# A reversed second token block, and a convolution DFT on sums and differences of the two blocks

## The chip, the cores and the metric

The kernel runs on one core of a Trainium2 chip. The metric is the device time of one execution in microseconds (us), the median of the runs. All of the work on tensors is on the device; the host only lays out the inputs, among them tables of sines and cosines, and puts the output's rows in order.

## The reference, cut to what matters

One decoder layer with 256 tokens of width 1024: RMS norm, an input projection, attention with 8 heads beside a convolution branch of 512 channels, an output projection with a residual, a second RMS norm and a SwiGLU of width 2816 with a residual. The change is in the convolution branch:

```python
def conformer_conv(u, glu_b, dw_w, dw_b, ln_g, ln_b):
    u = u + glu_b.astype(u.dtype)
    a, g = jnp.split(u, 2, axis=-1)
    h = a * jax.nn.sigmoid(g)
    h = jnp.pad(h, ((0, 0), (CONV_KERNEL - 1, 0), (0, 0)))
    h = lax.conv_general_dilated(
        h, dw_w[:, None, :].astype(h.dtype), window_strides=(1,), padding='VALID',
        dimension_numbers=('NWC', 'WIO', 'NWC'), feature_group_count=CONV_WIDTH)
    h = h + dw_b.astype(h.dtype)
    h = layer_norm(h, ln_g, ln_b)
    return jax.nn.silu(h)
```

It is a causal convolution with 31 taps along the tokens, for each channel by itself.

## The kernel before, in words

The tokens lie on the 128 partitions in two blocks: tokens 0 to 127 and 128 to 255. Every float32 product is made of three matmuls: an operand is split into a rounded high part and a low part (`split`, L207: ScalarE copies the high part, VectorE subtracts for the low one), and `mm3` (L318 to L321) adds high·high, high·low and low·high into one PSUM bank. A weight arrives in blocks of 2048 columns (`raw`) and is split piece by piece, 1024 columns each: `feed` (L275) issues the high part `wh` of a piece on ScalarE (L279) one piece ahead of the low part `wl` on VectorE (L227), and after the low part of an odd piece it loads a new block on SyncE's queue (L205). There is one stream of instructions for each engine, in the order of the program text; nothing is put in another order later. Generators (`spawn`, `step`) weave the side work into the matmul stream: one `step` for each group of six matmuls, and `yield n` means "go on n steps later". The constants at the top say how many steps.

The input projection (L739) runs over five chunks of 512 columns: k, q, the convolution's gate, the convolution's values, v. `conv_task` (L619) starts behind the fourth chunk and works beside the fifth. It forms the gated input `ua0`, `ua1` of the two blocks, splits them into `hh`, `hl`, and multiplies by `fwd`: a DFT of 256 tokens at odd frequencies whose cosine half goes to the bank `hf0` and whose sine half to `hf1` (`spectrum`, L637), each over both blocks. A third, short transform `hf2` takes block 1 alone: the wrapped-around part of the circular convolution is put right with it. `combine` multiplies by the spectra `Ws` of the taps, giving `Y0`, `Y1`; `Y2` comes from `hf2`. `ln_task` (L674) goes back with `inv`: one bank `cv` for each block, over Y0 and Y1, and Y2 for block 0. Then come the mean and variance (`bn_stats`), an inverse square root by small VectorE steps (`lr`, `nb`), `yn` on ScalarE, the transposes `cT` (L714), SiLU, and the split into `mix`, which the output projection `po` (L785) reads.

Beside this runs attention. For each head h there are scores `S`, a masked maximum `sm`, `bi` (VectorE), the exponentials `p` (ScalarE, L591), `rec` (VectorE), a scaling by GpSimd (L599), three transposes into a bank `pT` (L603) and a copy `pTs` out of it (ScalarE, L605). `pT` and `hf2` take turns in the two PSUM banks of the tag "t" (L158); `S` of heads 6 and 7, `hf0`, `hf1` and `cv` in the two of the tag "s". After head 7's exponentials ScalarE loads the table for SiLU (L594). Behind the chunks come `vs`, the values of v scaled (block 0 on ScalarE, L746, block 1 on VectorE, L747), the short transform (`third`, L658), and the products `O` of all heads (L759, L760), which need `vs` and the `pTs`.

After the output projection, `x2_task` (L788) adds the residual, transposes (`xT`, L801) and makes the next operand `g` (L807, L809), which the gate and up products `fg`, `fu` read (L308, L310).

Of the kernel before, what the change touches and what calls it, by code (L numbers as in the profile page):

```python
# [82 lines left out]

def _constants():


# [4 lines left out]
    c, s = waves(T, np.arange(T))  # L91
    ct, st = waves(2 * LAGS, np.arange(P) - (P - LAGS))
    fwd = np.concatenate([c[:P], s[:P], c[P:], s[P:], np.where(np.arange(P)[:, None] < P - LAGS, 0.0,
                                                              np.concatenate([ct, st, ct, st], 1))], 1)
# [47 lines left out]
def _build(nc, tc, t, ctx):  # L142
# [476 lines left out]
    def conv_task(banks):  # L619
        hh = early.tile([P, NT, W], F32R, name="hh", tag="hh")  # L620
        hl = early.tile([P, NT, W], F32R, name="hl", tag="hl")
        us = []
        for i in range(NT):
# [3 lines left out]
            nc.scalar.activation(hh[:, i, :], u, AF.Copy)  # L627
# [4 lines left out]
        nc.vector.tensor_tensor(hl[:, 1, :], us[1], hh[:, 1, :].bitcast(F32), op=ALU.subtract)  # L632
# [471 lines left out]
```

## Time and profile before

| what | us |
|---|---|
| median of 3 runs | 284.97 (284.8 to 285.31) |
| the profiled execution, first to last instruction (span) | 283.1 |
| TensorE busy / weight loads | 278.5 / 234.3 |
| VectorE busy | 239.0 |
| ScalarE busy | 207.8 |
| GpSimd busy | 47.7 |

The page of the profile gives no time of its own for the profiled execution beside its span. The median of the runs is 1.9 us above that span: what lies before the first and after the last instruction, and the scatter of the runs.

How to read the rows: PE is TensorE's matmuls, PEld its weight loads, DVE VectorE, ACT ScalarE, POOL GpSimd, SPq SyncE's DMA queue. A row of the timeline has the start, the length, engine, line, operation, output<-inputs, shapes and a count, and in brackets the idle time ahead of it with what ended that. A row of the chain has start, length, what. An instruction can show a start before its forerunner's end, since they are pipelined: the distance from start to start is what one of them costs in a row of them. Granted TensorE clock is 1.000 throughout.

### The profile page before, as it was taken

The page shows a single profiled execution, that of the slowest core. Times are in us where ns is not written, and L with a number is a line of the kernel's source. Part 1 is how long each engine was busy: PE and PEld are TensorE (multiplying, and loading weights), DVE is VectorE, ACT ScalarE, POOL GpSimd, SP SyncE. Part 2 cuts the span into 40 slices and gives each one's busy share as a digit, 9 for nine tenths or more (in the row PEclk, how much of TensorE's full clock was granted, in tenths as well). Part 3 has the DMA queues.
Part 4 walks back from the last instruction along what each step waited for, and adds up shares of the span by engine and source line. Part 5 has one row for each costly group of instructions (what it writes and reads, how often), then busy time and mean ns, then how long its engine had stood idle before and what let it go on. Part 6 is the DMA issues. An engine that isn't in the chain of part 4 may idle for free.

```text
span 283.1 us, 4174 instructions
## 1 busy us (share of the span) xinstructions
PE 278.5 (98%) x1463; PEld 234.3 (83%) x1463; DVE 239.0 (84%) x425; ACT 207.8 (73%) x336; POOL 47.7 (17%) x75
## 2 busy tenths in 40 slices
PE   8999999999999999999999999999999999999994
PEld 6788887788788888888888888888888888888883
DVE  3979996996894869999967687698789879999995
ACT  4858579996738677467878778776678799888770
POOL 0004556623000000000111111000011211211233
PEclk9999999999999999999999999999999999999999
DMA  7999957845203982659699998995686969999643
GB/s 247 396 425 354 420 191 275 328 160 214 85 7 141 362 316 78 287 163 394 202 291 280 304 318 228 285 274 171 243 213 167 242 183 258 321 311 207 190 74 148
DMA packets 13638, 69.03 MB, mean 244 GB/s; under 512 B 1777, under 2 KB 2385, under 8 KB 7730
## 3 DMA queue, kind: packets, MB, share of 16 engines
q1 hardware_dynamic: 10162, 56.19, 53.0%
q0 software_dynamic: 3312, 12.58, 22.1%
q8 instruction: 11, 0.18, 0.2%
q14 instruction: 9, 0.07, 0.1%
q10 hardware_dynamic: 144, 0.00, 0.0%
HBM read 66.15 MB, written 2.10 MB: 241 GB/s over the span
## 4 chain that ended last, share of the span: by engine, by line
PE 97%; DMA 1%; ACT 0%; DVE 0%; issue 0%
PE p L739 20%; PE sum L968 18%; PE fg L308 14%; PE fu L308 14%; PE po L785 8%; PE fg L310 7%; PE fu L310 7%; DMA first<-first 1%; PE S L561 1%; PE pT L603 1%; PE O L759 1%; PE xT L801 1%; PE cv L319 0%; PE cv L320 0%; PE hf L319 0%; PE cv L321 0%
## 5 line engine op out<-in xcount | busy, mean ns | idle before, releaser
L279 ACT ACTIVATE wh<-raw 128x1024 fp32r<-128x1024 f32 x81 | 83.9, 1053 | 15.3 <-PE fu L308 7.5
L227 DVE TENSOR_TENSOR wl<-raw,wh 128x1024 fp32r<-128x1024 f32 x63 | 75.9, 1219 | 3.4 <-ACT wh L279 3.3
L308 PE MATMUL fu<-g,wh 128*128 128x512 f32 x176 | 62.5, 395 | 0.0
L308 PE MATMUL fg<-g,wh 128*128 128x512 f32 x176 | 62.4, 394 | 0.0
L310 PE MATMUL fg<-g,wl 128*128 128x256 f32 x176 | 48.8, 277 | 0.0
L310 PE MATMUL fu<-g,wl 128*128 128x256 f32 x176 | 48.8, 277 | 0.0
L308 PEld LDWEIGHTS fg<-g,wh 128*128 128x128 f32 x176 | 33.0, 187 | 7.8
L308 PEld LDWEIGHTS fu<-g,wh 128*128 128x128 f32 x176 | 33.0, 188 | 7.6
L225 POOL DMA_DIRECT2D wl<-w x18 | 15.8, 876 | 138.2 <-ACT wl L224 74.3
L310 PEld LDWEIGHTS fg<-g,wl 128*128 128x128 f32 x176 | 33.0, 188 | 0.0
L310 PEld LDWEIGHTS fu<-g,wl 128*128 128x128 f32 x176 | 33.0, 188 | 0.0
L968 PE MATMUL sum<-wh,forms 128*128 128x512 f32 x96 | 29.6, 389 | 0.0
L739 PE MATMUL p<-wh,xh 128*128 128x512 f32 x80 | 25.7, 403 | 0.1
L739 PE MATMUL p<-wl,xh 128*128 128x512 f32 x80 | 24.8, 391 | 0.0
L739 PE MATMUL p<-wh,xl 128*128 128x512 f32 x80 | 24.7, 390 | 0.0
L279 ACT ACTIVATE wh<-t 128x1024 fp32r<-128x1024 f32 x18 | 19.1, 1059 | 6.0 <-DVE t L242 3.3
L227 DVE TENSOR_TENSOR wl<-t,wh 128x1024 fp32r<-128x1024 f32 x17 | 20.8, 1223 | 1.2 <-ACT wh L279 0.8
L968 PEld LDWEIGHTS sum<-wh,forms 128*128 128x128 f32 x96 | 17.9, 188 | 3.7
L224 ACT ACTIVATE wl<-wh 128x1024 fp32r<-128x1024 f32 x19 | 20.2, 1062 | 0.6
L968 PE MATMUL sum<-wl,forms 128*128 128x512 f32 x48 | 18.7, 389 | 0.0
L739 PEld LDWEIGHTS p<-wl,xh 128*128 128x128 f32 x80 | 14.9, 188 | 3.4 <-DVE wl L388 0.3
L739 PEld LDWEIGHTS p<-wh,xl 128*128 128x128 f32 x80 | 15.0, 188 | 3.3
(208 smaller groups left out, 475.6 us busy)
## 6 DMA issues: line engine op xcount, KB each, us to landing
raw<-w SPq DMA_DIRECT2D x44, 1024.0 KB, 6.8
wl<-w POOLq DMA_DIRECT2D x18, 512.0 KB, 9.5
first<-first SPq DMA_DIRECT2D x8, 384.0 KB, 6.3
raw<-w SPq DMA_DIRECT2D x2, 512.0 KB, 7.1
xtok<-xtok SPq DMA_DIRECT2D x2, 512.0 KB, 9.1
x<-xtok SPq DMA_DIRECT2D x2, 512.0 KB, 6.7
kept<-x POOLq DMA_DIRECT2D x1, 1024.0 KB, 4.1
raw<-kept SPq DMA_DIRECT2D x1, 1024.0 KB, 7.4
```

Source lines behind the costliest of these rows:

```text
L224: nc.scalar.activation(dst[1], dst[0].bitcast(F32), AF.Copy, scale=-1.0)
L225: nc.gpsimd.dma_start(dst[1], src.bitcast(F32R), accum_op=ALU.add)
L227: nc.vector.tensor_tensor(dst[1], src, dst[0].bitcast(F32), op=ALU.subtract)
L279: nc.scalar.activation(dst[0], src, AF.Copy)
L308: nc.tensor.matmul(out.rearrange("p (a q) -> p a q", a=2), w[0], both, start=z in first and z not in seen, stop=False)
L310: nc.tensor.matmul(out[:, 0:T], w[1], both[:, 0, :], start=False, stop=z in last and left[z] == 0)
L561: nc.tensor.matmul(banks[a][:, out], G["qT"][rows, j, q], G["kT"][rows, j, k], start=True, stop=True)
L603: nc.tensor.transpose(b[:, a * P:(a + 1) * P], p[:, a * P:(a + 1) * P], ident)
L739: nc.tensor.matmul(banks[i], (xh, xh, xl)[a][:, kt, sls[i]], w[a % 2], start=kt == 0 and a == 0, stop=kt == KT - 1 and a == 1)
L759: nc.tensor.matmul(o, vs[:, 0, hs], G["pT"][h][:, 0:T], start=True, stop=False)
L785: nc.tensor.matmul(po[i, n], G["mix"][l][:, k, i * P:(i + 1) * P], w[r], start=k == a == 0, stop=k == KT - 1 and a == 2)
L968: nc.tensor.matmul(banks[m], lhs, rhs, start=first, stop=last)
```

## The change

The tokens of block 1 are laid out in the order 128, 255, 254 ... 129 (`_turned`), in x, in the rotation table, in the mask and, on the host, in the output. Row r of block 1 (r from 1) then holds token 256-r, for which the DFT's cosines are those of token r with the sign changed and its sines the same. So the cosine half needs only the difference `ue` of the blocks and the sine half only their sum `uo` (row 0 apart: the columns `keep` and `minus` are 0 there). Forward there are three products of three matmuls, back three more, and the blocks are put together from `cv0` (even) and `cv1` (odd) on VectorE. That is 18 matmuls where there were 30.

```diff
-PT_WAIT = (4, 5, 3, 3)
+PT_WAIT = (4, 5, 5, 3)
-LN_WAIT = 2
+LN_WAIT = 3
-V_PIECE = 21
+V_PIECE = 22
...
+def _turned(a):
+
+    return np.concatenate([a[:P + 1], a[:P:-1]], 0)
...
     def conv_task(banks):
-        hh = early.tile([P, NT, W], F32R, name="hh", tag="hh")
-        hl = early.tile([P, NT, W], F32R, name="hl", tag="hl")
+        hh = early.tile([P, 3, W], F32R, name="hh", tag="hh")
+        hl = early.tile([P, 3, W], F32R, name="hl", tag="hl")
+        low = lambda j, u: nc.vector.tensor_tensor(hl[:, j, :], u, hh[:, j, :].bitcast(F32), op=ALU.subtract)
...
-            nc.scalar.activation(hh[:, i, :], u, AF.Copy)
             us.append(u)
-            if i:
-                nc.vector.tensor_tensor(hl[:, 0, :], us[0], hh[:, 0, :].bitcast(F32), op=ALU.subtract)
             yield 1
-        nc.vector.tensor_tensor(hl[:, 1, :], us[1], hh[:, 1, :].bitcast(F32), op=ALU.subtract)
+        ue, uo = work("ue", "tmp", 6), work("uo", "tmp", 6)
+        nc.vector.scalar_tensor_tensor(ue, us[1], G["minus"], us[0], op0=ALU.mult, op1=ALU.add)
+        nc.scalar.activation(hh[:, 0, :], ue, AF.Copy)
+        nc.vector.scalar_tensor_tensor(uo, us[0], G["keep"], us[1], op0=ALU.mult, op1=ALU.add)
+        nc.scalar.activation(hh[:, 1, :], uo, AF.Copy)
+        low(0, ue)
+        low(1, uo)
         yield HF_WAIT
...
-            for i in range(NT) if j < 2 else (1,):
-                o = i * T + j * P if j < 2 else 2 * T
-                mm3(b[:n, :], [f[:, o:o + n] for f in fwd], (hh[:, i, :], hl[:, i, :]), i == 0 or j == 2, i == NT - 1)
+            mm3(b[:n, :], [f[:, o:o + n] for f in fwd], (hh[:, j, :], hl[:, j, :]), True, True)
...
         combine(0)()
+        nc.scalar.activation(hh[:, 2, :], us[1], AF.Copy)
+        low(2, us[1])
         second = combine(1)
...
     def ln_task():
-        for i in (1, 0):
-            b = t_bank(f"cv{i}", "s")
-            for j in range(2):
-                o = j * T + i * P
-                mm3(b, [m[:, o:o + P] for m in inv], G["ys"][j], j == 0, i == 1 and j == 1)
-            if i == 0:
-                mm3(b, [m[:TAIL + 1, 2 * T:] for m in inv], G["ys"][2], False, True)
-                cv[i] = b
-            else:
-                cv[i] = work("cvb", "tmp", 6)
-                nc.vector.tensor_tensor(cv[i], b, G["glub"][:, 2, :], op=ALU.add)
+        for j in (1, 0, 2):
+            b = sums[j] = t_bank(f"cv{j}", "s" if j < 2 else "t")
+            n = TAIL + 1 if j == 2 else P
+            mm3(b, [m[:n, j * P:(j + 1) * P] for m in inv], G["ys"][j], True, True)
+        odd, even, late = (work(f"cv{a}", "tmp", 6) for a in "oel")
+        nc.vector.tensor_tensor(odd, sums[1], G["glub"][:, 2, :], op=ALU.add)
+        nc.scalar.activation(even, sums[0], AF.Copy)
+        nc.vector.scalar_tensor_tensor(late, even, G["minus"], odd, op0=ALU.mult, op1=ALU.add)
+        nc.vector.scalar_tensor_tensor(even, odd, G["keep"], even, op0=ALU.mult, op1=ALU.add)
+        nc.vector.tensor_tensor(even, sums[2], even, op=ALU.add)
+        cv = [even, late]
+        for i in (1, 0):
             nc.vector.bn_stats(st[:, i, :], cv[i])
             nc.vector.bn_aggr(mv[:, i, :], st[:, i, :])
-            if i:
-                feed(V_PIECE + 1)
```

The tables `fwd` and `inv` shrink from 1264 and 1280 columns to 752 and 768; the small table `cols` grows from 16 to 18. `V_PIECE` is the last piece whose low part is made during the v chunk. The order of the instructions moves at three places; the lines of the changed kernel are 6 to 14 higher than before.

TensorE from the first transform to the products O, before (`p40` is the v chunk's bank for block 0, six matmuls a group; `pT4` is head 4's bank):

```order
L321 MATMUL hf0_807<-hh_676,fwd_434 128x512
L603 MATMUL pT4_814<-c_ident_165,p4_712 128x128 x3
L603 MATMUL pT5_820<-c_ident_165,p5_721 128x128 x3
L739 MATMUL p40_662<-wh18_613,xh_110 128x512
...
L319 MATMUL hf1_836<-hh_676,fwd_434 128x512
...
L739 MATMUL p40_662<-wh19_642,xh_110 128x512
...
L603 MATMUL pT6_858<-c_ident_165,p6_778 128x128 x3
L603 MATMUL pT7_864<-c_ident_165,p7_791 128x128 x3
...
L319 MATMUL hf2_880<-hh_676,fwd_434 120x512
...
L759 MATMUL O0_895<-pTs0_668,vs_876 64x256
```

The same place with the change:

```order
L327 MATMUL hf0_811<-hh_676,fwd_434 128x512
L753 MATMUL p40_662<-wh18_613,xh_110 128x512
...
L325 MATMUL hf1_825<-hh_676,fwd_434 128x512
...
L753 MATMUL p40_662<-wh19_642,xh_110 128x512
...
L610 MATMUL pT4_850<-c_ident_165,p4_711 128x128 x3
L610 MATMUL pT5_856<-c_ident_165,p5_720 128x128 x3
L610 MATMUL pT6_862<-c_ident_165,p6_782 128x128 x3
L610 MATMUL pT7_868<-c_ident_165,p7_795 128x128 x3
...
L325 MATMUL hf2_884<-hh_676,fwd_434 120x512
...
L773 MATMUL O0_899<-pTs0_668,vs_880 64x256
```

`hf0` and `hf1` have three matmuls instead of six, and the transposes of heads 4 and 5 have moved two groups later, right ahead of those of heads 6 and 7. The four `pT` take turns in two banks.

ScalarE from head 7's last exponential to `vs`, before (`wh22` is the high part of weight piece 22):

```order
L591 ACTIVATE p7_791,sums_507<-sm7_750,bi7_754,scq_432 128x256
L594 ACT_TABLE_LOAD
L594 ACTIVATE table_76<-const-float32-1.0 128x1
L279 ACTIVATE wh22_795<-raw11_582 128x1024
L605 ACTIVATE pTs4_818<-pT4_814 128x384
L605 ACTIVATE pTs5_824<-pT5_820 128x384
```

With the change:

```order
L598 ACTIVATE p7_795,sums_507<-sm7_754,bi7_758,scq_432 128x256
L601 ACT_TABLE_LOAD
L601 ACTIVATE table_76<-const-float32-1.0 128x1
L285 ACTIVATE wh22_799<-raw11_582 128x1024
L285 ACTIVATE wh23_829<-raw11_582 128x1024
L667 ACTIVATE hh_676<-ua1_723 128x512
L612 ACTIVATE pTs4_854<-pT4_850 128x384
L612 ACTIVATE pTs5_860<-pT5_856 128x384
```

`wh23`, which came later in `ln_task`, and the third split's high part now stand between the table load and the copies `pTs4`, `pTs5`.

VectorE from the low part of piece 21 to `Y1`, before (`ya`, `yb` are the two products of `combine`):

```order
L227 TENSOR_TENSOR wl21_757<-raw10_493,wh21_756 128x1024
L597 RECIPROCAL rec7_826<-sums_507 128x2
L651 TENSOR_TENSOR ya0_849<-hf0_807,Ws_503 128x512
L652 TENSOR_TENSOR yb0_850<-hf1_836,Ws_503 128x512
L653 TENSOR_TENSOR Y0_544<-ya0_849,yb0_850 128x512
L651 TENSOR_TENSOR ya1_854<-hf0_807,Ws_503 128x512
L652 TENSOR_TENSOR yb1_855<-hf1_836,Ws_503 128x512
L747 TENSOR_SCALAR vs_876<-p41_663,c_176 128x512
L653 TENSOR_TENSOR Y1_545<-ya1_854,yb1_855 128x512
```

With the change:

```order
L233 TENSOR_TENSOR wl21_761<-raw10_493,wh21_760 128x1024
L604 RECIPROCAL rec7_815<-sums_507 128x2
L233 TENSOR_TENSOR wl22_800<-raw11_582,wh22_799 128x1024
L662 TENSOR_TENSOR ya0_839<-hf0_811,Ws_503 128x512
L663 TENSOR_TENSOR yb0_840<-hf1_825,Ws_503 128x512
L664 TENSOR_TENSOR Y0_544<-ya0_839,yb0_840 128x512
L629 TENSOR_TENSOR hl_677<-ua1_723,hh_676 128x512
L662 TENSOR_TENSOR ya1_846<-hf0_811,Ws_503 128x512
L663 TENSOR_TENSOR yb1_847<-hf1_825,Ws_503 128x512
L761 TENSOR_SCALAR vs_880<-p41_663,c_176 128x512
L664 TENSOR_TENSOR Y1_545<-ya1_846,yb1_847 128x512
```

`wl22` (from `ln_task`) and the third `hl` now stand ahead of `vs`. Earlier on VectorE, `ue` and `uo` stand between `ua1` and the first two `hl`, and the maxima of heads 6 and 7 follow those. Six matmuls of the output projection move from behind the transposes `cT` to ahead of them (36 instead of 30 ahead, 42 instead of 48 between `cT` and `xT`).

More of the change, by code (lines that the diff above doesn't have):

```diff
@@ L89, in waves @@
         return np.cos(ang), -np.sin(ang)
[L91 to L94, printed above, removed]
+    row = np.arange(P)
+    c, _ = waves(T, row)
+    _, s = waves(T, np.where(row == 0, P, row))
+    ct, st = waves(2 * LAGS, LAGS - row)
+    fwd = np.concatenate([c, s, np.where((row < 1) | (row > LAGS), 0.0, np.concatenate([ct, st, ct, st], 1).T).T], 1)
     fwd = _parts(fwd.astype(np.float32))
-    ir, ii = waves(2 * LAGS, np.arange(P) + LAGS)
-    tail = np.concatenate([ir, -ir, ii, ii], 1).T / LAGS * (np.arange(P) < LAGS)
-    tail = np.concatenate([tail, np.ones((1, P)), np.zeros((P - TAIL - 1, P))], 0)
+    ir, ii = waves(2 * LAGS, row + LAGS)
+    tail = np.concatenate([ir, -ir, ii, ii], 1).T / LAGS * (row < LAGS)
+    tail = np.concatenate([tail, (row == 0)[None], np.zeros((P - TAIL - 1, P))], 0)
     inv = _parts(np.concatenate([c.T * 2 / T, s.T * 2 / T, tail], 1).astype(np.float32))
@@ L107, in _constants @@
     out = {"fwd": fwd, "inv": inv, "taps": taps}
-    q, k = np.arange(P)[:, None], np.arange(P)[None, :]
-    tri = np.where(k <= q, 0.0, -1e30)
-    out["mask"] = np.concatenate([tri, np.zeros((P, P)), tri], 1).astype(np.float32)
+    at = _turned(np.arange(T))
+    tri = [np.where(b[None, :] <= b[:, None], 0.0, -1e30) for b in (at[:P], at[P:])]
+    out["mask"] = np.concatenate([tri[0], np.zeros((P, P)), tri[1]], 1).astype(np.float32)
     out["ident"] = np.eye(P, dtype=np.float32)
@@ L452, in tables_task @@
         G["glub"] = load(early, "rows", [P, 3, W])
-        G["cols"] = load(const, "cols", [P, 16])
+        G["cols"] = load(const, "cols", [P, 18])
+        G["keep"], G["minus"] = G["cols"][:, 16:17], G["cols"][:, 17:18]
     def spectra_task():
@@ L542, in q_task @@
         nc.gpsimd.tensor_scalar(G["scq"], cqk[0], HD ** -0.5, None, op0=ALU.mult)
-        for name, shape in (("fwd", [P, 2, 2 * T + TAIL]), ("inv", [P, 2, 2 * T + P])):
+        for name, shape in (("fwd", [P, 2, 2 * P + TAIL]), ("inv", [P, 2, 3 * P])):
             tl = early.tile(shape, F32R, name=name)
@@ L679, in ln_task @@
         vv = early.tile([P, NT], F32, name="vv")
-        for i in (1, 0):
-            b = t_bank(f"cv{i}", "s")
-            for j in range(2):
-                o = j * T + i * P
-                mm3(b, [m[:, o:o + P] for m in inv], G["ys"][j], j == 0, i == 1 and j == 1)
-            if i == 0:
-                mm3(b, [m[:TAIL + 1, 2 * T:] for m in inv], G["ys"][2], False, True)
-                cv[i] = b
-            else:
-                cv[i] = work("cvb", "tmp", 6)
-                nc.vector.tensor_tensor(cv[i], b, G["glub"][:, 2, :], op=ALU.add)
+        sums = {}
+        for j in (1, 0, 2):
[9 more added lines that the diff above has]
+        cv = [even, late]
+        for i in (1, 0):
             nc.vector.bn_stats(st[:, i, :], cv[i])
             nc.vector.bn_aggr(mv[:, i, :], st[:, i, :])
-            if i:
-                feed(V_PIECE + 1)
         nc.vector.tensor_scalar(vv, mv[:, :, 1], EPS, None, op0=ALU.add)
@@ L1053, in _layout @@
     A = {k: np.asarray(v) for k, v in a.items()}
-    x = A["x"][0]
+    x = _turned(A["x"][0])
     w_in = A["w_in"][0]
@@ L1081, in _layout @@
         "g1": colize(A["norm1_g"][0]),
-        "cols": np.concatenate([colize(A["norm2_g"][0]), colize(A["conv_ln_g"][0]), colize(A["conv_ln_b"][0])], 1),
+        "cols": np.concatenate([colize(A["norm2_g"][0]), colize(A["conv_ln_g"][0]), colize(A["conv_ln_b"][0]),
+                                np.outer(np.arange(P) > 0, np.float32([1, -1]))], 1).astype(np.float32),
         "rows": rep(np.concatenate([A["glu_b"][0].reshape(2, W), A["dw_b"]], 0)),
@@ L1102 @@
     o = np.asarray(r.results[0]["out"])
-    return np.ascontiguousarray(o).reshape(1, T, D)
+    return np.ascontiguousarray(_turned(o)).reshape(1, T, D)
```

5 lines of the change are left out of this document (2 added, 3 removed).

## Prediction

> **What bounds the kernel now.** I read the page's busy times first, then what TensorE waits for, then the chain that ended last, and then the timelines of TensorE, VectorE and ScalarE around the convolution.
>
> From the page, and from the view of TensorE's waits, its only row:
>
> ```profile
> PE 278.5 (98%) x1463; PEld 234.3 (83%) x1463; DVE 239.0 (84%) x425; ACT 207.8 (73%) x336; POOL 47.7 (17%) x75
> PE warm L370 <- PEq L1095: 0.8, 1, 0.8
> ```
>
> TensorE is busy for 98% of the span and stands idle for nothing but the warm-up's start. So the span of before is TensorE's stream, and any change ends it earlier by what it takes out of that stream, less the waits that it puts in. The chain of waits, between 60 and 106 us, shows the stretch in question (start, length, what):
>
> ```profile
> 63.01 0.23 PE hf L319
> ...
> 69.89 1.37 PE p L739 x6
> ...
> 74.92 0.43 PE cv L319
> ...
> 78.39 0.23 PE cv L321
> 78.63 6.83 PE po L785 x30
> 85.46 0.87 PE cT L714 x8
> 86.33 10.93 PE po L785 x48
> 97.26 0.87 PE xT L801 x8
> ...
> 105.94 0.32 PE fg L308
> ```
>
> One matmul of the transforms costs 0.233 us in the stream (14 steps from 74.92, its first a little longer, to 78.39: 0.23 each), one of the output projection 6.83/30 = 0.228, a group of six of the v chunk 1.37.
>
> **What the change takes out.** Twelve transform matmuls at 0.233 make 2.80 us, 1.40 in `hf` and 1.40 in `cv`. If TensorE stayed the bound, that would be the gain, whole. [...] The stage at hand tells another story, by the view of busy times from the end of `ua1` to two us past `vs` (stretch, length, then PE, PEld, DVE, ACT, POOL busy with their counts, the granted clock, and DMA):
>
> ```profile
> 59.68:74.10 14.42, 14.42 (x88) 11.88 (x88) 11.54 (x28) 11.45 (x26) 4.12 (x8) 1.00 0.47 181
> ```
>
> VectorE has 14.42 - 11.54 = 2.9 us free here, and the change brings `ue`, `uo` (about 0.65 each in a row), the third `hl` (0.60) and `wl22` (1.12): 3.0 us. The room is just used up if nothing waits. So the question is what waits.
>
> **VectorE's slip at the split.** The timelines of VectorE and ScalarE before:
>
> ```profile
> 58.21 0.74 DVE L625 SCALAR_TENSOR_TENSOR ua<-p,c,c_rows 128x512 f32<-128x512 f32 x1
> 58.99 0.69 DVE L626 TENSOR_TENSOR ua<-ua,sgt 128x512 f32<-128x512 f32 x1
> ...
> 60.42 0.69 DVE L632 TENSOR_TENSOR hl<-ua,hh 128x512 fp32r<-128x512 f32 x1
> ...
> 62.97 1.22 DVE L227 TENSOR_TENSOR wl<-raw,wh 128x1024 fp32r<-128x1024 f32 x1
> ...
> 64.18 1.20 DVE L227 TENSOR_TENSOR wl<-raw,wh 128x1024 fp32r<-128x1024 f32 x1
> 64.11 0.15 DVE L597 RECIPROCAL rec<-sums 128x2 f32<-128x2 f32 x1
> 65.30 0.15 DVE L597 RECIPROCAL rec<-sums 128x2 f32<-128x2 f32 x1
> ...
> 67.89 0.69 DVE L652 TENSOR_TENSOR yb<-hf,Ws 128x512 f32<-128x512 f32 x1 [1.85 <-PE hf L321]
> 68.62 0.69 DVE L653 TENSOR_TENSOR Y<-ya,yb 128x512 f32<-128x512 f32 x1
> 69.23 0.68 DVE L651 TENSOR_TENSOR ya<-hf,Ws 128x512 f32<-128x512 f32 x1
> ...
> 71.30 0.75 DVE L747 TENSOR_SCALAR vs<-p,c 128x512 f32<-128x512 f32 x1 [0.79 <-PE p L739]
> ```
>
> ```profile
> 59.78 0.61 ACT L627 ACTIVATE hh<-ua 128x512 fp32r<-128x512 f32 x1
> 60.30 1.05 ACT L279 ACTIVATE wh<-raw 128x1024 fp32r<-128x1024 f32 x1
> ...
> 62.33 0.49 ACT L591 ACTIVATE p<-sm,bi,scq 128x128 f32<-128x128 f32 x1 [0.24 <-DVE bi L586]
> ...
> 64.59 1.28 ACT L594 ACT_TABLE_LOAD   x1
> 65.88 0.20 ACT L594 ACTIVATE table<-const-float32-1.0 128x1 f32<-128x1 f32 x1
> 65.99 1.05 ACT L279 ACTIVATE wh<-raw 128x1024 fp32r<-128x1024 f32 x1
> 66.94 0.85 ACT L605 ACTIVATE pTs<-pT 128x384 f32<-128x384 f32 x2
> ```
>
> `ua1` ends at 59.68. `ue` follows at 59.72 (0.04 from end to start, as L625 to L626). No row has this operation from SBUF alone; the nearest are L625, which reads PSUM (0.74), and L626 (0.69), and I take 0.71. Then `hh0` on ScalarE (0.61, from 60.47), `uo` meanwhile to 61.09, `hh1` to 61.74, and only then the second `hl`, at 61.78 and not 60.42: a slip of 1.36 us. Behind it stand the `rec` and the maxima of heads 6 and 7, whose exponentials waited for VectorE already (the bracket at 62.33). So all of ScalarE's row slips by 1.36: table load 67.22 done, `wh22` at 67.35, done at 68.40.
>
> **VectorE's wait for `wh22`.** VectorE is through `rec7` at 65.45 + 1.36 = 66.81, then stands at `wl22`, which needs `wh22`: it starts at 68.44, a new wait of some 1.6 us. Behind it: `ya0` 1.12 later (64.18 to 65.30) at 69.56, `yb0` 0.60, `Y0` 0.73 (67.89 to 68.62), `hl` 0.61, then three steps of 0.60 to `vs` at 73.30, which ends at 74.05. Before it ended at 71.30 + 0.75 = 72.05: 2.00 later. The products `O` need it from their second matmul on, and `cv` follows `O`. With the first product already through, I take `cv` 1.95 us later than 74.92, give or take 0.4.
>
> **TensorE meanwhile** has its own new wait, and it is covered by this one. `hf0` must also wait until the maximum has read head 6's bank (0.2). `pT4` then comes at 63.01 + 0.2 + 2 x 0.70 + 2 x 1.37, about 67.4, and `pT5` is through 0.66 later; `pT6` needs `pT4`'s bank, so the copy `pTs4`, which stands behind `wh22`, `wh23` (0.95 from start to start, 65.99 to 66.94) and `hh` (0.52, 59.78 to 60.30): from 69.77 to 70.24. TensorE stands there for 2.2 us, finishes `hf2` near 73.1 and waits once more, 0.9, for `vs`. Were this first wait gone, `vs` would still be late.
>
> **At the output projection**: +1.95 - 1.40 (the six `cv` matmuls) = **+0.55**. Beside the `po` matmuls runs the way to `yn`:
>
> ```profile
> 76.56 0.69 DVE L690 TENSOR_TENSOR cvb<-cv,c_rows 128x512 f32<-128x512 f32 x1 [0.28 <-PE cv L321]
> ...
> 82.34 0.16 DVE L698 SCALAR_TENSOR_TENSOR nb<-mv,lr 128x2 f32<-128x2 f32 x1
> ...
> 83.22 0.80 ACT L703 ACTIVATE yn<-cvb,nb,lr 128x512 f32<-128x512 f32 x1
> ```
>
> From the first addition to `nb` it took 82.50 - 76.56 = 5.94, with one `wl` of 1.12 in it, and 1.52 more to the end of `yn`. That `wl` is gone, and three operations of some 0.73 are added (two to put the blocks together, one for the third bank). It starts once `O` is split, about 1.3 (a `hh`-like copy and a subtraction) behind its end near 76.9: 78.2 + 5.94 - 1.12 + 2.2 + 1.52 = 86.7. `cT` is due at 85.46 + 0.55 + 6 x 0.228 = 87.38. So this work costs nothing, with 0.6 to spare; beyond that each us would count.
>
> **Behind `cT`** it has slipped by 0.55 + 1.37 = 1.92, and what hangs on it is tight:
>
> ```profile
> 89.27 0.69 DVE L209 TENSOR_TENSOR mixl<-cs,mixh 128x512 fp32r<-128x512 f32 x1 [0.88 <-ACT mixh L208]
> 89.88 5.76 DVE L227 TENSOR_TENSOR wl<-raw,wh 128x1024 fp32r<-128x1024 f32 x5
> 95.56 1.28 DVE L791 TENSOR_TENSOR x<-po,x 128x512 f32<-128x512 f32 x2
> ...
> 105.22 1.66 DVE L809 SCALAR_TENSOR_TENSOR g<-xT,c_cols,g 128x256 fp32r<-128x256 f32 x4 [1.77 <-ACT g L807]
> ```
>
> From `mixl` to the residual VectorE has no idle time, and 42 matmuls instead of 48 lie over it. The residual ends at 96.84 + 1.92 = 98.76; `xT`'s second half would be due at 97.26 + 0.43 + 0.55 = 98.24: a wait of about 0.5. The same holds at the second `xT`, and the fifth `g` (ready 105.22 + 0.42 = 105.64, used at 105.94) has 0.30 of slack. So the end slips by 1.92 - 0.30 = **+1.6**. Behind that the trace of before shows TensorE without a wait.
>
> **Edits at nothing.** The smaller tables come on GpSimd's queue at 45 us, far ahead of their use at 63 and 75; `cols` has two columns more; the row order is the host's. Piece 23's low part and the block load behind it on SyncE's queue come at 86.4 instead of 83.6:
>
> ```profile
> 83.66 12.34 SPq L205 DMA_DIRECT2D raw<-w  x4
> raw<-w SPq DMA_DIRECT2D x44, 1024.0 KB, 6.8
> ```
>
> The block lands 6.8 later, at 93.2; ScalarE reads it as the last of five high parts, near 94.9 with its own slip. Covered by 1.7; uncovered, it would delay the weights of the gate product.
>
> **The sum** against the profiled execution: -2.80 of matmuls, +3.35 of waits ahead of `cv` (1.95 + 1.40), +1.05 from `xT` on: 283.1 becomes 284.7. The runs' median is 1.9 above that span, and nothing is changed at either end: 284.97 + 1.6 = 286.6.
>
> **The rivals.**
>
> *The second half is hidden* (chance 0.20). For: the slacks behind `cT` come from single rows. Against: three places in a row are tight. Then only +0.55 is left: 285.5, with 285.0 to 285.9.
>
> *VectorE's new work fits its free time* (0.18), the case on the other side. Place: `wl22`. If `wh22` is done by the time VectorE has passed `rec7`, near 66.7, the 1.6 us of wait and most of the slip go, `vs` ends within 0.2 us of before, and `po` starts 1.2 earlier. Against: `wh22` stands behind the table load, and that behind VectorE itself. And the chain behind `cT` would take back up to 1.1 of it. 283.7 to 284.8.
>
> *TensorE stays the bound* (0.06), -2.80: 282.2. The 2.9 us of free time against 3.0 of new work and two waits speak against it.
>
> *The clock falls in the new gap* (0.06). The stretch above shows a granted clock of 1.00, but TensorE has no wait in it. If the 2.2 us ahead of `pT6` brought it to half, the nine matmuls up to `O` would take twice their 0.23, 2.1 more, of which the 0.9 of waiting for `vs` hides a part: +1.2 on the forecast, 287.8. [...]
>
> **How the numbers follow.** The forecast keeps 0.50, with 285.9 to 287.4 as its own range (0.4 of `vs`, 0.3 of slack). The range 284.1 to 287.5 takes in the forecast, the hidden second half and two thirds of the fitting case; left out are that case's last third, the full gain and the fallen clock, 0.06 each. A measurement of this kernel tells about 0.2% from no change, 0.57 us. Slower by more than that: the forecast, the fallen clock and half of the hidden case, 0.66. Faster by more: two thirds of the fitting case and the full gain, 0.18. Within: the rest of these two cases, 0.16.
>
> **What would show it.** In the profile after: `wl22` on VectorE with an idle time of 1 to 2 us ahead of it that ScalarE's `wh` ends; `vs` on VectorE ending near 74; TensorE with a row of waits for `pTs` or `vs`, and one at `xT`; `po` starting near 79.2, `cT` near 87.4. The forecast is wrong if TensorE shows no waits between 63 and 106 us, or if `po` starts before 78.

## The result and the profile after

| kernel | median of 6 runs, us | lowest and highest | ratio to before |
|---|---|---|---|
| before | 284.97 | 284.8 to 285.45 | |
| changed | 287.0 | 286.73 to 288.8 | 1.0088 (95% interval 1.0070 to 1.0106) |

The change makes the kernel 2.0 us slower. The six runs of the changed kernel fall into two groups: four at 286.73 to 287.04 with a mean granted clock of 0.998 to 1.000, and two at 288.66 and 288.8 with 0.994. The profiled execution is the 288.8: its span is 286.7, and those of the four are 284.9 to 285.3.

The page's busy times and the view of TensorE's waits, after:

```profile
PE 279.2 (97%) x1451; PEld 235.2 (82%) x1451; DVE 242.9 (85%) x431; ACT 209.0 (73%) x338; POOL 47.7 (17%) x75
PE pT L610 <- ACT pTs L612: 2.1, 1, 2.1
PE warm L376 <- PEq L1110: 0.8, 1, 0.8
PE xT L815 <- DVE x L805: 0.4, 1, 0.4
PE hf L325 <- ACT pTs L612: 0.3, 1, 0.3
```

Twelve matmuls are gone and three waits are new. They stand in the forecast with 2.2, 0.5 and 0.2 us. For the third the profile names ScalarE's copies `pTs`, and the forecast the maximum of head 6, which ends at 63.91, 0.11 ahead of `hf0`; which of the two `hf0` waits for isn't shown. The timeline of VectorE, from the sums to `vs`:

```profile
60.42 0.75 DVE L640 SCALAR_TENSOR_TENSOR ue<-ua,c_cols,ua 128x512 f32<-128x512 f32 x1
61.09 0.75 DVE L642 SCALAR_TENSOR_TENSOR uo<-ua,c_cols,ua 128x512 f32<-128x512 f32 x1
61.87 0.69 DVE L629 TENSOR_TENSOR hl<-ue,hh 128x512 fp32r<-128x512 f32 x1
62.54 0.69 DVE L629 TENSOR_TENSOR hl<-uo,hh 128x512 fp32r<-128x512 f32 x1
...
67.42 0.15 DVE L604 RECIPROCAL rec<-sums 128x2 f32<-128x2 f32 x1
69.18 1.22 DVE L233 TENSOR_TENSOR wl<-raw,wh 128x1024 fp32r<-128x1024 f32 x1 [1.61 <-ACT wh L285]
...
74.90 0.75 DVE L761 TENSOR_SCALAR vs<-p,c 128x512 f32<-128x512 f32 x1 [0.77 <-PE p L753]
```

`wl22` waits 1.61 us for `wh22`, as forecast. But `vs` waits 0.77 for TensorE, which the forecast does not have. The view of busy times in four stretches around TensorE's wait says why (stretch, length, then PE, PEld, DVE, ACT, POOL, the granted clock, DMA):

```profile
69.00:71.10 2.10, 0.07 (x1) 0.00 (x0) 1.92 (x3) 2.10 (x5) 0.02 (x1) 1.00 0.90 359
71.10:71.80 0.70, 0.66 (x5) 0.62 (x6) 0.67 (x2) 0.38 (x2) 0.00 (x0) 0.88 0.92 386
71.80:75.20 3.40, 3.40 (x11) 2.72 (x10) 2.63 (x5) 1.56 (x3) 0.00 (x0) 0.52 0.72 292
75.20:78.00 2.80, 2.80 (x31) 2.43 (x31) 2.80 (x6) 2.26 (x4) 0.00 (x0) 1.00 0.00 0
```

TensorE is idle from 69 to 71.1, and some 0.5 us after it goes on its granted clock falls to half for 3.4 us. This is the rival of the fallen clock, in this execution. To read the rest without it I use the second experiment below, which differs only in that the transposes of heads 4 and 5 stand one group earlier. Its clock is 1.000 throughout, and its `cv`, `po` and first residual stand where those of two more kernels with a held clock stand, to within 0.02 us.

The start of the input projection differs from one execution to the next. Its first two pairs of matmuls take 0.74 and 0.63 us in the profile before, but 1.21 and 1.05 in the one after, and in the ninth experiment TensorE waits twice in this projection, 1.2 in all, for the high part of a weight. So the rows of two executions are offset by up to 1.2 us. All milestones are therefore counted from the first scores matmul `S` (44.52 in the profile before, 45.14 in the second experiment, 45.23 after; 44.33 in the third at the earliest, 45.54 in the ninth at the latest). From the timelines, in us:

| kernel | `vs` ends | `cv` | `po` | `nb` ends | `cT` | `cs` | first `x` | fifth `g` used | end | end - `x` |
|---|---|---|---|---|---|---|---|---|---|---|
| before | 27.53 | 30.34 | 33.95 | 37.98 | 40.78 | 41.46 | 51.04 | 61.26 | 238.58 | 187.54 |
| after, clock fallen | 30.42 | 33.23 | 35.44 | 41.87 | 43.63 | 44.32 | 53.89 | 64.05 | 241.47 | 187.58 |
| 2: clock held | 29.55 | 32.36 | 34.56 | 41.00 | 42.74 | 43.43 | 53.00 | 63.17 | 240.56 | 187.56 |
| 1: `V_PIECE` 21 | 28.04 | 30.85 | 33.04 | 40.62 | 41.53 | 43.03 | 52.58 | 62.74 | 240.16 | 187.58 |
| 3: `LN_WAIT` 2 | 29.56 | 32.36 | 34.57 | 41.01 | 41.92 | 43.42 | 52.98 | 63.15 | 240.57 | 187.59 |
| 4: `hf` doubled | 29.56 | 32.37 | 34.57 | 41.02 | 42.75 | 43.44 | 53.02 | 63.19 | 240.71 | 187.69 |
| 5: `wl25` earlier | 29.56 | 32.36 | 34.56 | 41.00 | 42.74 | 43.43 | 52.22 | 62.39 | 239.77 | 187.55 |
| 6: no assembly | 29.55 | 32.36 | 34.57 | 39.51 | 41.40 | 42.08 | 51.66 | 61.85 | 239.21 | 187.55 |
| 7: 21, piece 25 earlier | 28.03 | 30.84 | 33.04 | 40.61 | 41.52 | 42.86 | 51.64 | 61.82 | 239.34 | 187.70 |
| 8: before, order alone | 27.52 | 30.33 | 33.94 | 37.97 | 40.75 | 41.43 | 51.01 | 61.23 | 238.53 | 187.52 |
| 9: before, `wl25` earlier | 27.53 | 30.34 | 33.94 | 37.97 | 40.76 | 41.44 | 50.71 | 61.24 | 238.56 | 187.85 |
| 10: no sums | 28.75 | 31.56 | 33.76 | 40.20 | 41.96 | 42.64 | 52.22 | 62.39 | 239.85 | 187.63 |
| 11: four edits | 28.04 | 30.84 | 33.05 | 39.49 | 41.22 | 41.90 | 50.70 | 61.24 | 238.75 | 188.05 |
| 12: longer wait | 31.50 | 34.52 | 36.72 | 43.16 | 44.90 | 45.59 | 55.17 | 65.34 | 242.70 | 187.53 |

A `+` below is a milestone that comes later than before. With the clock held the change brings `cv` +2.02, `po` +0.61, `cT` +1.96, the first residual +1.96, the fifth `g` +1.91, the end +1.98. The medians agree: the four runs with a held clock have a median of 286.94, 1.97 over before. No profile of the changed kernel itself with a held clock was taken; up to `po` experiment 3, whose waits ahead of that are the changed kernel's, shows the same milestones as experiment 2.

### The profile page after: what moved, and what is told of

The parts are those of the page before. It is cut to its first block, busy times and chain, and to the rows that moved or that the text cites. A ratio compares the mean times of both kernels' runs of the same rounds, so it can differ in the third digit from the quotient of the medians.

```text
span 286.7 us, 4163 instructions
## 1 busy us (share of the span) xinstructions
PE 279.2 (97%) x1451; PEld 235.2 (82%) x1451; DVE 242.9 (85%) x431; ACT 209.0 (73%) x338; POOL 47.7 (17%) x75
## 4 chain that ended last, share of the span: by engine, by line
PE 85%; ACT 7%; DVE 4%; issue 2%; DMA 1%; ACTq 0%; DVEq 0%
PE sum L982 18%; PE p L753 17%; PE fg L314 14%; PE fu L314 14%; PE fg L316 7%; PE fu L316 7%; PE po L799 3%; ACT wh L285 3%; DMA first<-first 1%; PE S L568 1%; ACT sq L809 1%; ACT p L598 1%; PE O L773 1%; ACT cs L731 1%; DVE g L823 1%
## 5 line engine op out<-in xcount | busy, mean ns | idle before, releaser
L753 PE MATMUL p<-wh,xh 128*128 128x512 f32 x80 | 26.6, 414 | 0.1
L753 PE MATMUL p<-wh,xl 128*128 128x512 f32 x80 | 25.6, 402 | 0.0
L753 PEld LDWEIGHTS p<-wh,xl 128*128 128x128 f32 x80 | 15.6, 195 | 3.5
L753 PEld LDWEIGHTS p<-wl,xh 128*128 128x128 f32 x80 | 15.6, 195 | 3.4
```

Of the source, the lines that this page charges most:

```text
L753: nc.tensor.matmul(banks[i], (xh, xh, xl)[a][:, kt, sls[i]], w[a % 2], start=kt == 0 and a == 0, stop=kt == KT - 1 and a == 1)
```

## Experiments

The first four were made on the theory of the prediction.

**1. Piece 22's low part back between the two `bn_stats`.**

```diff
-V_PIECE = 22
+V_PIECE = 21
...
             nc.vector.bn_aggr(mv[:, i, :], st[:, i, :])
+            if i:
+                feed(V_PIECE + 1)
```

> The changed kernel with piece 22's low part and piece 23's high part left where they were before the change (V_PIECE 21, the feed in ln_task). My theory: VectorE no longer waits 1.6 us for wh22 ahead of ya0, hh and pTs4 come 0.95 earlier on ScalarE, so vs on VectorE ends near 72.3 instead of 74.05 on the clock of before, cv starts 0.2 later than before and not 1.95, and po 1.2 earlier than before. The low part is back in the way to yn, so cT waits about 0.5 and slips by 0.65 against before, and the end by 0.35: 285.3 us, 1.7 less than the changed kernel (ratio to before 1.001). TensorE's wait for pTs falls from 2.1 to about 1.3, so the clock does not fall. Rival, the second half behind cT is hidden: 283.8 (ratio 0.996). Rival, TensorE's wait for the pT bank alone is what costs: about 0.9 less than the changed kernel, 286.1.

Measured: 287.01 (286.67 to 287.19), ratio 1.0066 (1.0052 to 1.0079). A miss. The first half came: `vs` ends 1.51 and `po` starts 1.52 earlier than in experiment 2, and `po` is even 0.91 earlier than before. But the end gains only 0.40 against experiment 2 (0.29 by the medians), where 1.7 against the changed kernel was expected. `wl22` now stands on the way from `cv` to `nb`, which ends only 0.38 earlier.

**2. The transposes of heads 4 and 5 one group earlier.**

```diff
-PT_WAIT = (4, 5, 5, 3)
+PT_WAIT = (4, 5, 4, 3)
```

> The changed kernel with the transposes of heads 4 and 5 one step earlier (PT_WAIT 4 instead of 5 for that pair), so pTs4 and pTs5 come ahead of wh23 and hh on ScalarE, and the 2.1 us wait ahead of pT6 shrinks to about 0.8. My theory: that wait was covered by VectorE's late vs; the time that TensorE gains it loses again ahead of hf2 (waits for hl, 1.3) and O (1.1). cv starts where it did: 286.9 us, ratio to before 1.007, and as the single gaps are shorter the clock falls in fewer runs. Rival, the pT wait sets the end: 2.0 less, 284.9 (ratio 1.000).

Measured: 287.3 (286.91 to 287.74), ratio 1.0076 (1.0062 to 1.0089). The view of TensorE's waits:

```profile
PE hf L326 <- DVE hl L629: 0.7, 1, 0.7
PE pT L610 <- ACT pTs L612: 0.6, 1, 0.6
PE O L774 <- DVE vs L761: 0.5, 1, 0.5
PE xT L815 <- DVE x L805: 0.4, 1, 0.4
```

The one wait of 2.1 has become three (`hl` and `O` with 0.7 and 0.5, where 1.3 and 1.1 were expected), and nothing is won: TensorE's wait ahead of `pT6` lies beside VectorE's way to `vs`, as the prediction had it. No run shows a fallen clock. The rival, that this wait itself costs 2 us, is out.

**3. `cT` one group earlier.**

```diff
-LN_WAIT = 3
+LN_WAIT = 2
```

> The changed kernel with LN_WAIT 2, so that 30 and not 36 matmuls of the output projection stand ahead of cT. My theory: cT is due 0.55 later than before, at 86.0, yn is done at 86.7, so TensorE waits 0.5 to 0.7 there; but the chain mix, residual, xT, g then slips by 1.25 and not 1.92, its waits behind cT nearly go, and the end comes about 0.35 sooner than with the change: 286.6, ratio 1.0055. Rival, the slacks behind cT hide the second half: then the added group ahead of cT costs nothing, and taking it away adds the wait at cT: 0.6 more than with the change, 287.5.

Measured: 287.22 (286.76 to 288.35), ratio 1.008 (1.006 to 1.0099). A miss: against experiment 2 `cT` starts 0.82 earlier, `cs` 0.01, and the end stays where it was. ScalarE's timeline shows why:

```profile
85.38 0.81 ACT L717 ACTIVATE yn<-cve,nb,lr 128x512 f32<-128x512 f32 x1 [5.44 <-DVE nb L712]
86.10 0.80 ACT L717 ACTIVATE yn<-cvl,nb,lr 128x512 f32<-128x512 f32 x1
86.80 1.04 ACT L285 ACTIVATE wh<-raw 128x1024 fp32r<-128x1024 f32 x1
87.75 0.99 ACT L731 ACTIVATE cs<-cT,c_cols 128x256 f32<-128x256 f32 x2
```

Behind `nb` there is no idle time left: `yn`, `yn`, the high part of piece 25, `cs`. That high part (0.95) stands between `yn` and `cs`, and the prediction had not counted it.

**4. `hf0` and `hf1` computed twice.**

```diff
-            mm3(b[:n, :], [f[:, o:o + n] for f in fwd], (hh[:, j, :], hl[:, j, :]), True, True)
+            for _ in range(2 if j < 2 else 1):
+                mm3(b[:n, :], [f[:, o:o + n] for f in fwd], (hh[:, j, :], hl[:, j, :]), True, True)
```

> The changed kernel with the three matmuls of hf0 and of hf1 made twice each into the same bank (the second time starting it anew), six more matmuls or 1.40 us of TensorE's work, as many as the change took out there. My theory: they only fill TensorE's wait ahead of pT6 (2.1 becomes 0.7), for wl22 and vs do not hang on them: no more than 0.2 beside the changed kernel, 286.9 to 287.1, and with the gap gone the clock does not fall, so all runs lie there. Rival, TensorE's stream sets the end in this stretch: +1.4, 288.4.

Measured: 287.35 (287.04 to 287.67), ratio 1.008 (1.0066 to 1.0094). TensorE's wait ahead of `pT6` shrinks from 2.1 to 0.7, and `po` stands at 34.57 as without the 1.4 us of matmuls. So in the changed kernel the six matmuls that it saves in `hf` are worth nothing.

After these four the theory was: what sets the end is the row `nb`, `yn`, `wh25`, `cs`, `mixl`, five low parts, first residual `x`, and a fixed way from there on. These are ScalarE's and VectorE's rows of experiment 2, the latter from the second `mixl` to the second residual:

```profile
86.18 0.82 ACT L717 ACTIVATE yn<-cve,nb,lr 128x512 f32<-128x512 f32 x1 [5.44 <-DVE nb L712]
86.90 0.80 ACT L717 ACTIVATE yn<-cvl,nb,lr 128x512 f32<-128x512 f32 x1
87.61 1.04 ACT L285 ACTIVATE wh<-raw 128x1024 fp32r<-128x1024 f32 x1
88.57 1.02 ACT L731 ACTIVATE cs<-cT,c_cols 128x256 f32<-128x256 f32 x2
```

```profile
90.28 0.69 DVE L215 TENSOR_TENSOR mixl<-cs,mixh 128x512 fp32r<-128x512 f32 x1 [1.87 <-ACT mixh L214]
91.86 0.69 DVE L215 TENSOR_TENSOR mixl<-cs,mixh 128x512 fp32r<-128x512 f32 x1 [0.88 <-ACT mixh L214]
92.47 5.76 DVE L233 TENSOR_TENSOR wl<-raw,wh 128x1024 fp32r<-128x1024 f32 x5
98.14 1.28 DVE L805 TENSOR_TENSOR x<-po,x 128x512 f32<-128x512 f32 x2
...
103.19 1.66 DVE L823 SCALAR_TENSOR_TENSOR g<-xT,c_cols,g 128x256 fp32r<-128x256 f32 x4 [0.51 <-ACT g L821]
104.76 1.28 DVE L805 TENSOR_TENSOR x<-po,x 128x512 f32<-128x512 f32 x2
```

**5. The low part of piece 25 ahead of the first `mixl`,** where VectorE stands idle for 1.87.

```diff
             feed(off + k + lead(0, 2 * k + n))
+            if 2 * k + n == 5:
+                feed(off + k + 3, 0)
```

> The changed kernel with one low part, that of piece 25, taken out of the five behind the second mixl on VectorE and put ahead of the first mixl, where VectorE stands idle for 1.9 us. Theory after the first runs: behind cs VectorE's row (mixl, five low parts at 1.12, the first residual x) sets the time of xT and of g, so the residual comes 1.12 earlier, TensorE's wait at xT (0.8 with its weight loads) and at the fifth g (0.5) goes, and the end comes 0.9 to 1.2 earlier: 285.9, ratio to before 1.003. Rival (the loss comes wholly from cs, which comes late, and the low parts are paced by their transfers and ScalarE): 287.0, ratio 1.007.

Measured: 287.32 (286.28 to 287.64), ratio 1.0064 (1.0047 to 1.0082). The median is no test here, because the clock fell in four of the six runs (287.02 to 287.64, 0.994); the two others took 286.28 and 286.3. The profile of one of these two shows the first residual and the end 0.8 earlier than in experiment 2, a little less than the 0.9 to 1.2 expected:

```profile
91.35 0.69 DVE L215 TENSOR_TENSOR mixl<-cs,mixh 128x512 fp32r<-128x512 f32 x1 [0.88 <-ACT mixh L214]
92.30 4.63 DVE L233 TENSOR_TENSOR wl<-raw,wh 128x1024 fp32r<-128x1024 f32 x4 [0.26 <-ACT wh L285]
96.85 1.28 DVE L805 TENSOR_TENSOR x<-po,x 128x512 f32<-128x512 f32 x2
```

There are four low parts instead of five, with 0.26 of waiting for a high part. VectorE's row sets the residual, and the residual the end. The rival is out.

**6. Without the assembly of the blocks, and `cT` one group earlier.**

```diff
-LN_WAIT = 3
+LN_WAIT = 2
...
-        nc.vector.scalar_tensor_tensor(late, even, G["minus"], odd, op0=ALU.mult, op1=ALU.add)
-        nc.vector.scalar_tensor_tensor(even, odd, G["keep"], even, op0=ALU.mult, op1=ALU.add)
         nc.vector.tensor_tensor(even, sums[2], even, op=ALU.add)
-        cv = [even, late]
+        cv = [even, odd]
```

> The changed kernel with LN_WAIT 2 (cT one group earlier, which alone gave nothing), and without the two operations that put the blocks together: the even and the odd half are normalized as they are, so the convolution's values are not the reference's. Theory: the way from cv over the assembly and nb to yn, and behind it wh25 on ScalarE, sets cs; 1.5 us less on that way bring yn ahead of cT's place, cs comes about 1.0 earlier and so does the end: 286.0 to 286.2, ratio 1.004. Rival (what holds cs is not yn, or what holds the residual is not cs): 287.2, ratio 1.008.

Measured: 286.35 (285.57 to 287.17), ratio 1.0039 (1.0021 to 1.0057), with a fallen clock in three of seven runs. `nb` ends 1.50 earlier than in experiment 3, `cs` starts 1.34 and the end comes 1.36 earlier. With experiment 3 this shows that `nb`, and what ScalarE does behind it, holds `cs`. That TensorE's place for `cT` holds it at the same time is read from the table: `cs` starts 0.69 behind `cT` in experiment 2, as close as before (0.68) and here (0.68). No run brings `nb` earlier with `cT` left in its place and nothing else changed.

**7. Piece 22 as in 1, and both parts of piece 25 put where their engines are idle.**

```diff
-V_PIECE = 22
+V_PIECE = 21
...
             nc.vector.bn_aggr(mv[:, i, :], st[:, i, :])
+            if i:
+                feed(V_PIECE + 1)
...
-            feed(off + k + lead(0, 2 * k + n))
+            feed(off + k + (lead(0, 2 * k + n) if (k, n) != (1, 0) else 3))
+            if 2 * k + n == 4:
+                feed(off + k + 3, 0)
```

> The changed kernel with V_PIECE 21 (the low part of piece 22 goes back between the two bn_stats, as in the first run), the high part of piece 25 ahead of yn on ScalarE, where it is idle for 5 us, and the low part of piece 25 ahead of the first mixl on VectorE. Theory: the first run brought po 0.9 earlier than before and lost it again behind nb; with both pieces out of the way TensorE keeps most of it, po to xT without a wait: 0.4 to 0.9 under before, 284.3, ratio 0.998. Rival (the longer way through nb holds cs all the same): 286.5, ratio 1.005.

Measured: 285.9 (285.45 to 286.47), ratio 1.0027 (1.0017 to 1.0038). Between the theory's 284.3 and the rival's 286.5. Of the 1.98 by which the end came later, 1.22 is won back, but the first residual is still 0.60 later than before and the end 0.76. `nb` is still 2.63 later, and TensorE waits 0.4 at `cT` for `yn`, which stands behind it.

**8. The order of the tokens alone,** in the kernel before. The diff shows two of its edits; the tables of the transform, the mask and the rotation are turned in the same way.

```diff
-    c, s = waves(T, np.arange(T))
+    c, s = (_turned(m) for m in waves(T, np.arange(T)))
...
-    x = A["x"][0]
+    x = _turned(A["x"][0])
```

> The kernel before with the tokens of block 1 in the turned order and nothing else: 30 transform matmuls as before, with the rows and columns of their tables in that order. Theory: the order alone costs nothing, since no instruction changes: 285.0, ratio 1.000. Rival (the order has a price of its own, in the rotation, the mask or the layout): over 285.6.

Measured: 285.14 (284.78 to 285.54), ratio 1.0004 (0.9995 to 1.0014). It costs nothing, as expected; the milestones agree with those of before to within 0.05.

**9. The edit of experiment 5 in the kernel before,** one group earlier, as its `cT` is.

```diff
             feed(off + k + lead(0, 2 * k + n))
+            if 2 * k + n == 4:
+                feed(off + k + 3, 0)
```

> The kernel before (30 matmuls, no turned tokens) with the low part of piece 25 ahead of the first mixl, as in the run of the changed kernel with that edit. TensorE has no wait in this stretch of the kernel before, so the edit frees nothing: 284.9, ratio 1.000. Rival (the five low parts cost the kernel before as well, so the edit helps whatever the transform): 284.2, ratio 0.997 or less.

Measured: 285.23 (284.86 to 286.02), ratio 1.0007 (0.9998 to 1.0017). The residual comes 0.33 earlier and the end 0.02. So VectorE's row does not hold the end of the kernel before, but it is level with what does: its end lies 187.54 behind the residual, no farther than in kernels whose residual holds the end (187.55 in experiments 5 and 6). TensorE shows no wait in this stretch.

**10. Without `ue` and `uo`.**

```diff
-        ue, uo = work("ue", "tmp", 6), work("uo", "tmp", 6)
-        nc.vector.scalar_tensor_tensor(ue, us[1], G["minus"], us[0], op0=ALU.mult, op1=ALU.add)
+        ue, uo = us
         nc.scalar.activation(hh[:, 0, :], ue, AF.Copy)
-        nc.vector.scalar_tensor_tensor(uo, us[0], G["keep"], us[1], op0=ALU.mult, op1=ALU.add)
         nc.scalar.activation(hh[:, 1, :], uo, AF.Copy)
```

> The changed kernel without ue and uo: the blocks ua0 and ua1 go into the two transforms as they are, so the convolution is not the reference's. Theory: the sums set VectorE back by 1.36 us behind ua1, and with it the exponentials, the table load and wh22; without them wl22 and vs come 1.3 to 1.4 earlier, the copies pTs too (TensorE's wait ahead of pT6 falls from 2.1 to about 0.8, so its clock holds), cv, cT, nb and the residual move along, and the end comes 1.2 to 1.4 earlier: 285.6, ratio 1.002. Rival (ScalarE's row is held by its own work, and the sums stand in VectorE's free time): 286.9, ratio 1.007.

Measured: 286.8 (286.22 to 287.24), ratio 1.0059 (1.0044 to 1.0074). By the median this is next to the rival's 286.9, and the theory's 285.6 is missed. The milestones, which leave the offset of the start out, lie between the two: `vs`, `cv`, `nb` and the first residual come 0.78 to 0.80 earlier than in experiment 2, the end 0.71. VectorE's timeline shows what took the place of the sums:

```profile
59.31 0.69 DVE L634 TENSOR_TENSOR ua<-ua,sgt 128x512 f32<-128x512 f32 x1
60.75 1.29 DVE L629 TENSOR_TENSOR hl<-ua,hh 128x512 fp32r<-128x512 f32 x2 [0.75 <-ACT hh L640]
```

The first `hl` waits 0.75 for ScalarE's `hh`. Before the change that copy was made one group earlier, from `ua0`. So of the slip at the split 0.80 is the sums themselves, and 0.61 (`hl` at 16.51 against 15.90) is that both splits now stand behind `ua1`. The wait ahead of `pT6` fell only to 1.8 accordingly; the clock held in all six runs.

**11. Four edits together:** experiment 7, the low part of piece 22 made without VectorE, and pieces 30 and 31 one step later.

```diff
-            if i:
-                feed(V_PIECE + 1)
...
     nc.vector.tensor_scalar(vs[:, 1, :], banks[1], rstd1[:, 1:2], None, op0=ALU.mult)
+    dst, src, j = waiting.pop(0)
+    low_part(dst, home(j), True)
...
-            return LEAD if 0 < d < OUT_LATE else LEAD - 1
+            return (LEAD - 2 if d == 4 else LEAD) if 0 < d < OUT_LATE else LEAD - 1
```

> The changed kernel as in the run with V_PIECE 21 and both parts of piece 25 put earlier, and two things more: the low part of piece 22 is made without VectorE (ScalarE writes the negative of the high part behind vs, and a DMA on GpSimd's queue adds the weights to it), and the parts of pieces 30 and 31 come one step later, behind g and not ahead of it. Theory: in all kernels so far the end lies 187.6 us behind the first residual x, because x, ScalarE's squares, two high parts, g, the second residual, xT and g again follow one another; two high parts less (1.9) and a way to nb that is 1.1 shorter leave TensorE as the bound, with po 0.9 earlier than before: 284.2, ratio 0.997. Rivals: the DMA of the low part lands too late for the 25th matmul of po (median 9.3 us for its like in other places): 285.5 or more; or g is held by something else: 285.9 as in the run before.

Measured: 285.52 (284.98 to 287.44), ratio 1.0019 (1.0003 to 1.0035). `xT` starts at 51.67, 0.90 earlier than before (52.57), so the 0.90 that `po` had won arrives there whole. Then it is lost again. The timelines of VectorE and of TensorE:

```profile
98.59 1.66 DVE L825 SCALAR_TENSOR_TENSOR g<-xT,c_cols,g 128x256 fp32r<-128x256 f32 x4 [1.87 <-ACT g L823]
100.17 2.35 DVE L233 TENSOR_TENSOR wl<-raw,wh 128x1024 fp32r<-128x1024 f32 x2
102.44 1.28 DVE L807 TENSOR_TENSOR x<-po,x 128x512 f32<-128x512 f32 x2
```

```profile
103.18 1.25 PE L817 MATMUL xT<-c_ident,x 128*128 128x128 f32 x8 [0.23 <-DVE x L807]
105.99 0.50 PE L314 MATMUL fg<-g,wh 128*128 128x512 f32 x1 [0.15 <-DVE g L825]
```

The two low parts went from ahead of `g` to ahead of the second residual, and held that instead. The fifth `g` is used at 61.24, as before the change (61.26). A place behind the second residual was not tried. The time is the one that the first rival named (285.5), but not by its way: ScalarE has written the negative for piece 22's low part at 73.44, the 25th matmul of `po` starts at 83.24, and TensorE waits for nothing in `po`, so the DMA in between is not too late. One of the twelve runs took 287.44 at a clock of 1.000; why isn't known. No version here beats the kernel before.

**12. A longer wait ahead of `pT6`,** by ScalarE's copy made three times.

```diff
-        nc.scalar.activation(hh[:, 2, :], us[1], AF.Copy)
+        for _ in range(3):
+            nc.scalar.activation(hh[:, 2, :], us[1], AF.Copy)
```

> The changed kernel with ScalarE's copy hh of block 1 made three times instead of once, 1.05 us more ahead of the copy pTs4: TensorE's wait ahead of pT6 grows from 2.1 to 3.1 us. If the clock held, this would cost next to nothing, for vs ends at the same time as before: 287.2. Theory: the clock falls behind a wait with a chance that grows with its length (10 of 25 runs so far at 2.1 us, none of 28 at 1.1 or less), so now in most runs: 288.7, ratio 1.013. [...]

Measured: 289.54 (287.78 to 290.82), ratio 1.0159 (1.0129 to 1.0189). TensorE's wait is 3.4 us, and the clock fell in five of six runs, as in these stretches of the profiled one:

```profile
68.00:71.70 3.70, 0.32 (x3) 0.09 (x1) 3.21 (x5) 3.64 (x7) 0.30 (x1) 1.00 0.84 340
71.70:72.50 0.80, 0.76 (x7) 0.72 (x8) 0.80 (x2) 0.48 (x2) 0.00 (x0) 1.00 1.00 410
72.50:75.90 3.40, 3.40 (x11) 2.56 (x9) 1.56 (x3) 1.37 (x3) 0.00 (x0) 0.50 0.34 136
75.90:79.00 3.10, 3.10 (x34) 2.37 (x32) 3.10 (x7) 2.15 (x4) 0.00 (x0) 1.00 0.00 0
```

That fits the theory that the chance of a fall grows with the wait, though six runs are few: at the 10 in 25 of the shorter wait, five or more of six would come about once in 24 times. The run whose clock held (0.999) took 287.78, 0.6 over the expected 287.2; the wait was 0.3 longer than planned, and what the rest of the 0.6 is no profile of that run shows. The median is 0.8 over the theory's 288.7; two of the runs have a mean clock of 0.988, twice the usual loss of 0.006.

## Why the prediction was right, and where its sizes were off

The direction was right, and the mechanism in the main: +1.6 us forecast, 286.6 with a range of 284.1 to 287.5, and 287.0 or +2.0 measured. One step, the way to `yn`, came out right by luck, and one term, the slack at the fifth `g`, was mis-sized. By its steps:

- **The slip at the split.** Forecast 1.36 on the second `hl`, measured 1.41. `ue` and `uo` take 0.75 each, not 0.71. Experiment 10 divides it: only 0.80 of it belongs to the sums, the rest to the order of the splits.
- **The wait for `wh22`, and `vs`.** 1.6 forecast, 1.61 measured; `vs` +2.00 forecast, +2.02 measured. Experiment 1 takes `wl22` away from there and `vs` comes 1.51 earlier.
- **TensorE's wait ahead of `pT6`.** 2.2 forecast, 2.07 in the trace, and covered, as experiments 2 and 4 show. The second wait, for `vs`, was smaller than forecast: from the first product `O` to `cv` it is 3.54 us in experiment 3, against 2.98 before, so 0.56 and not 0.9. The rival in which TensorE stays the bound is out: 1.4 us of matmuls more at this place leave `po` where it is (experiment 4). That TensorE is the busiest engine, with 98%, said little: its weight loads are busy for 83% of the span before, and VectorE for 84%.
- **The output projection.** `po` +0.55 forecast, +0.61 measured.
- **The way to `yn`.** The forecast has it cost nothing, "with 0.6 to spare". The step looked at one consumer only, `cT`. It left out `wh25`, which stands between `yn` and `cs` on ScalarE. Before the change `cs` started 3.48 behind `nb`; the least that `yn`, `yn` and `wh25` allow is 2.43, so 1.05 was to spare there. `nb` has become 3.02 later: 2.02 from `cv`, and 1.00 from three added operations and a wait of 0.31 for ScalarE's copy, less `wl22`. That uses up the 1.05 and leaves 1.97, which happens to be the 1.96 by which `cT` is later. So this step was right by luck: a little more work ahead of `nb` would have cost time, and experiment 3 shows that an earlier `cT` brings nothing. The rows are ScalarE's before, where `cs` waited 1.01 behind `wh25`, and VectorE's in experiment 2, with the three added operations (L702 to L704); ScalarE's of experiment 2 are shown above.

```profile
83.92 1.04 ACT L279 ACTIVATE wh<-raw 128x1024 fp32r<-128x1024 f32 x1
85.98 1.02 ACT L717 ACTIVATE cs<-cT,c_cols 128x256 f32<-128x256 f32 x2 [1.01 <-issue]
```

```profile
79.83 0.75 DVE L702 SCALAR_TENSOR_TENSOR cvl<-cve,c_cols,cvo 128x512 f32<-128x512 f32 x1 [0.31 <-ACT cve L699]
80.62 0.75 DVE L703 SCALAR_TENSOR_TENSOR cve<-cvo,c_cols,cve 128x512 f32<-128x512 f32 x1
81.47 0.69 DVE L704 TENSOR_TENSOR cve<-cv,cve 128x512 f32<-128x512 f32 x1
...
85.98 0.16 DVE L712 SCALAR_TENSOR_TENSOR nb<-mv,lr 128x2 f32<-128x2 f32 x1
```

- **Behind `cT`.** The slip of 1.92 was right (first residual +1.96). The slack of 0.30 at the fifth `g` was not there: it is used 1.91 later. The prediction took it as the distance from when `g` is ready, 105.64, to where the chain shows its matmul, 105.94. In TensorE's timelines, of before and of experiment 2, the matmul starts at 105.78, and with the change it waits:

```profile
105.78 0.48 PE L308 MATMUL fg<-g,wh 128*128 128x512 f32 x1
```

```profile
108.31 0.50 PE L314 MATMUL fg<-g,wh 128*128 128x512 f32 x1 [0.17 <-DVE g L823]
```

So at most 0.14 was there, and of the 1.96 at the residual only 0.05 is gone at the fifth `g`. This term, 0.25 too large, is most of the 0.4 by which the forecast was low.
- **The rival of the second half.** It held that the slip behind `cT` is hidden. It is not: in twelve of the fourteen kernels in the table the end lies 187.5 to 187.7 behind the first residual, whatever was done ahead of it. The two others are those in which the residual comes earliest, at 50.70 and 50.71. There something else binds: the second residual in 11, and in 9 what bound the kernel before, whose end it shares.
- **The rival of VectorE's free time.** The price of the added work at the one place was right, but its free time was needed in order, not in sum: VectorE stood idle for 1.61 us ahead of `wl22`. Experiment 1 shows that its move back gives the gain at `po` (0.91 earlier than before) and takes it away behind `nb`.
- **The fallen clock.** Forecast with a chance of 0.06, an estimate that no run of before bears on: TensorE's only wait there is 0.8 at the warm-up. It fell in two of six runs. It was priced at +1.2, with the clock at half, which is what the profile shows (0.52 over 3.4 us). Counted from `S`, the profiled execution ends 0.91 later than experiment 2; between the fallen and the held spans of experiment 5 lie 0.8 to 1.3 (285.2 to 285.7 against 284.4). Between the two groups of the changed kernel lie 1.7 (286.7 against 285.0), but part of that can lie ahead of `S`, which came late in the profiled one (45.23); no profile of the other group shows how much.
- **Edits at nothing.** This held. In experiment 2 ScalarE's five high parts run without a wait, so the later block load is covered, and experiment 8 shows that the order of the tokens costs nothing.
